# Where the tiles of a two-layer encoder trunk begin in SBUF: five pads changed

## The chip, the core and the metric

The kernel runs on one core of one Trainium2 chip, in one launch. The metric is the device time of that launch in microseconds (us); lower is better. The time before is 1945.97 us, the median of three runs that lie between 1945.92 and 1946.1 us.

The engines are called by the names of the profile: PE is TensorE (the matrix unit), PEld the load of its stationary operand, DVE is VectorE, ACT is ScalarE, POOL is GpSimd, SP is SyncE, which issues the loads of the weights. A matrix product has two operands in SBUF: the *stationary* one, 128 columns that are loaded into the array beforehand, and the *moving* one, whose columns (256, 288 or 512 here) stream past it. While one product streams, the stationary operand of the next is loaded.

## The reference

Two layers over 256 tokens of width 2048, all float32. Layer 0 mixes tokens by a convolution module, layer 1 by multi-head latent attention; each is followed by a squared-ReLU MLP of width 8192.

```python
def conv_module(h, w_pw1, b_pw1, w_dw, b_dw, ln_g, ln_b, w_pw2, b_pw2):
    u = h @ w_pw1 + b_pw1
    a, gate = jnp.split(u, 2, axis=-1)
    u = a * jax.nn.sigmoid(gate)
    u = lax.conv_general_dilated(u, w_dw[:, None, :].astype(u.dtype),
        window_strides=(1,), padding=[(CONV_WIDTH - 1, 0)], feature_group_count=D_MODEL, ...) + b_dw
    u = jax.nn.silu(layer_norm(u, ln_g, ln_b))
    return u @ w_pw2 + b_pw2

def mla(h, cos, sin, w_in, q_norm_g, kv_norm_g, w_q_up, w_kv_up, w_o):
    c_q, c_kv, k_pe = jnp.split(h @ w_in, [512, 1024], axis=-1)
    q = rms_norm(c_q, q_norm_g) @ w_q_up
    kv = rms_norm(c_kv, kv_norm_g) @ w_kv_up
    ...
    return o @ w_o

def sq_relu_mlp(h, w1, w2):
    return jnp.square(jax.nn.relu(h @ w1)) @ w2

def reference(x, positions, ...):
    for layer in range(2):
        h = rms_norm(x, norm_mixer_g[layer])
        x = x + (conv_module(h, ...) if layer == 0 else mla(h, ...))
        h = rms_norm(x, norm_mlp_g[layer])
        x = x + sq_relu_mlp(h, mlp_w1[layer], mlp_w2[layer])
    return rms_norm(x, final_norm_g)
```

The depthwise convolution is 31 taps wide and looks back only. The attention has 16 heads with 128 + 64 query and key dimensions, of which the 64 are rotated by position, and 128 value dimensions; a token sees the tokens up to the end of its own chunk of 64.

## The kernel before, in words

**Three products for one.** To keep float32 accuracy each operand is split into a high part (rounded to the format `F32R`) and a low part (the rest), and each product is made as high·high + low·high + high·low. `mm3` (L192) issues the three where the activations are stationary and the weights move (L194 high activations with high weights, L195 low activations with high weights, L196 high activations with low weights). Where the weights are stationary and the activations move, the three stand in the loops of the stage itself.

**Weights.** SP loads each block of weights into a tile `raw` (three buffers); ACT writes its high part into a tile `hi`, DVE (in the convolution mostly POOL) the low part into a tile `lo`, six buffers of each (`WB`), so the splitting runs ahead of PE by up to six tiles.

**Activations.** `xt` holds the turned (transposed) and normalised tokens, four tiles `xt_1` to `xt_4` in a pool on the right end of SBUF; for each block k of 128 features the high part of 256 tokens lies beside the low part of the same tokens. `sh` and `sl_` hold the gated, convolved and turned rows in the convolution module; the tiles `sh`/`sl` and `gh`/`gl` of an MLP hold its squared hidden values. In the attention, `kvh`/`kvl` and `qh`/`ql` hold the compressed keys and queries, `kTh`/`kTl`, `qTh`/`qTl`, `qpA`, `qpB`, `kpA`, `kpB` the keys and queries of a group of four heads, `vv` and `pT` values and softmax weights, `oh`/`ol` the heads' outputs.

**Stages, in order of time.**

1. The first convolution product (`conv_mm`, L841; L847 to L849): weights stationary, 256 columns of `xt` moving, 1536 products, in 16 rounds of 96. Around it, by a hand-written order, DVE makes the 31 taps of the depthwise convolution (L949), POOL splits weights (L169). Then LayerNorm.
2. The second convolution product (L1169, then `product_A`): `sh`/`sl_` stationary, 512 columns of weights moving, 384 products.
3. The MLP of layer 0. Up: weights stationary, L509 moves `xhl(k)`, the 512 columns of both parts of `xt`, past the high weights, L507 moves the 256 columns of the high part past the low weights; 16 of each for 128 hidden features. Down: `sh`, `sl`, `gh`, `gl` stationary, 512 columns of weights moving (L194 to L196), partly in a form with seven block products in place of eight. The hidden width is cut into four quarters; the first quarter's up products run alone, then down products of one quarter alternate with up products of the next (`ORDERS`), and the last quarter's down products run alone.
4. The attention. Its first product makes `ckv` in two blocks of 288 columns (`NKV`, L1590) and then `cq` in one of 512 (L1604), with `xt` stationary. The products with `kvh`, `kvl`, `qh`, `ql` follow (256 columns; stationary or moving), the scores (L1515 to L1517), the values, and the output product with `oh`/`ol` stationary (512 columns).
5. The MLP of layer 1, and the last normalisation.

**Addresses.** Each pool lays its tiles one behind the other, so a pad, a tile that nothing reads, moves what is behind it. All `hi` and `lo` tiles begin at 64 modulo 256 bytes, and so do the slices of 128 or 512 columns that the products take from them. The right pools (`xt`, and in the attention `gp` with the keys, queries and values of the heads) end below `pad_right`, so its size sets where they begin. The numbers of the pads are counts of float32, 4 bytes each.

Of the kernel before, what the change touches and what calls it, by code (L numbers as in the profile page):

```python
# [10 lines left out]
F32 = mybir.dt.float32  # L11
# [7 lines left out]
P = 128  # L19
# [16 lines left out]
PARTS = 4  # L36
PAD_CONST = 24
PAD_SMALL = 32
PAD_RIGHT = 48
PAD_KV = 8  # L40
PAD_O = 56
WB = 6
LOOK = WB // 2 - 1
LAST_PE = 22
# [37 lines left out]
def trunk_kernel(  # L82
# [26 lines left out]
    nc = tc.nc  # L109
# [22 lines left out]
    edge = ctx.enter_context(tc.tile_pool(name="edge", bufs=1, side="right"))  # L132
    pad_right = edge.tile([P, PAD_RIGHT], F32, name="pad_right")
    nc.gpsimd.memset(pad_right, 0.0)
# [658 lines left out]
    with ExitStack() as cx:  # L793
        cv = cx.enter_context(tc.tile_pool(name="cv", bufs=1, reuse_waits="tile"))
# [12 lines left out]
        b2 = cv.tile([P, D], F32, name="b2")  # L807

        cn = cv.tile([P, T, D], F32, tag="tok", name="cn")
        sh = cv.tile([P, KC, S], F32R, name="sh")  # L810
        sl_ = cv.tile([P, KC, S], F32R, name="sl_")
        stats = cv.tile([P, T, KC // 2, 6], F32, name="stats")

        UC = 2
# [429 lines left out]
    with ExitStack() as cx:  # L1244
        at = cx.enter_context(tc.tile_pool(name="at", bufs=1, reuse_waits="tile"))
# [92 lines left out]
                if h == 1:  # L1338
                    u_load(u + 3)

        pad_kv = at.tile([P, PAD_KV], F32, name="pad_kv")
        nc.gpsimd.memset(pad_kv, 0.0)
        kvh = at.tile([P, KR // P, S], F32R, name="kvh")
        kvl = at.tile([P, KR // P, S], F32R, name="kvl")
        qh = at.tile([P, QR // P, S], F32R, name="qh")
# [15 lines left out]
        for i in range(2):  # L1361
            for j in range(HG):
                nc.scalar.activation(qpB[i][DR:, j, :], mq[DR:, :], AF.Copy)
        pad_o = at.tile([P, PAD_O], F32, name="pad_o")
        nc.gpsimd.memset(pad_o, 0.0)
# [413 lines left out]
```

## Time and profile before

| | |
|---|---|
| median of 3 runs | 1945.97 us |
| the profiled execution's own time | 1946.03 us |
| its span, first to last instruction | 1944.2 us |
| PE busy | 1919.3 us, 99% of the span, 10778 products |
| DVE busy | 1652.7 us, 85% |
| ACT busy | 1206.4 us, 62% |
| POOL busy | 223.9 us, 12% |
| granted clock of PE | 0.999 |
| loaded from HBM | 363.68 MB, 188 GB/s over the span |

The profile is one execution. A row of the groups of instructions gives how many there are, their busy time, and the mean length of one in nanoseconds. Products overlap in the array: a product of 512 columns is shown as some 390 ns long, though the next one starts after some 230 ns. So two numbers are of use: the distance from one start to the next in the timeline, and the difference between the shown lengths of two groups. Around the span the execution has 1.8 us.

### The profile page before, as it was taken

How to read it: one execution, taken by the hardware profiler on the slowest of the kernel's cores; microseconds unless marked ns; L12 is line 12 of the kernel's file. 1: busy time of each engine (PE TensorE's matmuls, PEld its weight loads, DVE VectorE, ACT ScalarE, POOL GpSimd, SP SyncE). 2: the span in 40 equal slices, each digit the busy share in tenths (PEclk: the TensorE clock that was granted, in tenths of full speed). 3: DMA queues.
4: the chain of work that ended last, by engine and by line, in shares of the span. 5: the costliest groups of instructions: out<-in, count | busy, mean ns of one | idle time of the engine just before them, and what ended most of it. 6: DMA issues, size and time to landing. Idle time of an engine off the chain costs nothing.

```text
span 1944.2 us, 28476 instructions
## 1 busy us (share of the span) xinstructions
PE 1919.3 (99%) x10778; PEld 1675.2 (86%) x10778; DVE 1652.7 (85%) x2372; ACT 1206.4 (62%) x1709; POOL 223.9 (12%) x184
## 2 busy tenths in 40 slices
PE   7999999999999999999999999999999999999998
PEld 7999888888888888888899998888888888888886
DVE  5999865789999999999976665657999999999887
ACT  5556654766666666666566665566666666666654
POOL 5999400000000000000001410000000000000000
PEclk9999999999999999999999999999999999999999
DMA  8666355856666667666645445765667666666663
GB/s 237 182 179 191 130 195 154 231 168 206 204 195 206 196 201 210 197 199 211 200 145 180 119 149 174 208 181 172 196 195 209 203 195 196 213 199 194 209 223 108
DMA packets 407113, 367.62 MB, mean 189 GB/s; under 512 B 15416, under 2 KB 351936, under 8 KB 406720
## 3 DMA queue, kind: packets, MB, share of 16 engines
q1 hardware_dynamic: 405952, 363.63, 62.4%
q10 hardware_dynamic: 1024, 2.17, 0.3%
q8 instruction: 84, 1.38, 0.3%
q14 instruction: 53, 0.43, 0.1%
HBM read 363.68 MB, written 2.10 MB: 188 GB/s over the span
## 4 chain that ended last, share of the span: by engine, by line
PE 96%; DVE 1%; ACT 1%; POOL 1%; DMA 1%; issue 0%; DVEq 0%; ACTq 0%; POOLq 0%
PE acc L509 25%; PE acc L194 15%; PE acc L195 15%; PE acc L196 15%; PE acc L507 12%; PE acc L849 3%; PE acc L848 3%; PE acc L847 3%; PE acc L250 1%; PE sum L897 1%; PE acc L1547 0%; POOL lo L169 0%; DMA xs<-in_x 0%; ACT hi L168 0%; PE acc L1411 0%
## 5 line engine op out<-in xcount | busy, mean ns | idle before, releaser
L420 DVE TENSOR_TENSOR lo<-raw,hi 128x1024 fp32r<-128x1024 f32 (+1 forms) x512 | 571.2, 1122 | 91.4 <-ACT hi L419 90.8
L419 ACT ACTIVATE hi<-raw 128x1024 fp32r<-128x1024 f32 (+1 forms) x512 | 479.7, 970 | 67.8 <-PE acc L195 67.3
L509 PE MATMUL acc<-xt,hi 128*128 128x512 f32 x2048 | 512.8, 396 | 0.0
L509 PEld LDWEIGHTS acc<-xt,hi 128*128 128x128 f32 x2048 | 375.6, 188 | 79.3
L194 PE MATMUL acc<-hi,sh 128*128 128x512 f32 x930 | 363.4, 391 | 0.0
L196 PE MATMUL acc<-lo,sh 128*128 128x512 f32 x930 | 362.2, 390 | 0.0
L195 PE MATMUL acc<-hi,sl 128*128 128x512 f32 x802 | 312.0, 389 | 0.0
L507 PEld LDWEIGHTS acc<-xt,lo 128*128 128x128 f32 x2048 | 260.2, 188 | 11.7
L507 PE MATMUL acc<-xt,lo 128*128 128x256 f32 x2048 | 262.5, 281 | 0.0
L168 ACT ACTIVATE hi<-raw 128x1024 fp32r<-128x1024 f32 (+2 forms) x184 | 180.0, 1005 | 46.9 <-PE acc L195 41.7
L196 PEld LDWEIGHTS acc<-lo,sh 128*128 128x128 f32 x930 | 174.6, 188 | 37.0
L194 PEld LDWEIGHTS acc<-hi,sh 128*128 128x128 f32 x930 | 174.6, 188 | 36.7
L169 DVE TENSOR_TENSOR lo<-raw,hi 128x1024 fp32r<-128x1024 f32 (+2 forms) x118 | 133.2, 1148 | 68.7 <-ACT hi L168 62.9
L419 ACT ACTIVATE hi<-V 128x1024 fp32r<-128x1024 f32 x94 | 99.6, 1059 | 127.3 <-DVE V L715 124.0
L195 PEld LDWEIGHTS acc<-hi,sl 128*128 128x128 f32 x802 | 150.6, 188 | 31.4
L949 DVE SCALAR_TENSOR_TENSOR sum<-ub,w_dw,sum 128x256 f32<-128x256 f32 x400 | 162.8, 480 | 7.6 <-ACT sum L905 6.5
L169 POOL TENSOR_TENSOR lo<-raw,hi 128x1024 fp32r<-128x1024 f32 x66 | 157.7, 2414 | 23.9 <-ACT hi L168 23.9
L514 ACT ACTIVATE U<-acc 128x512 f32<-128x512 f32 x128 | 76.2, 595 | 131.2 <-PE acc L509 130.9
L419 ACT ACTIVATE hi<-T 128x1024 fp32r<-128x1024 f32 x94 | 99.3, 1056 | 85.7 <-DVE T L703 79.9
L847 PE MATMUL acc<-xt,hi 128*128 128x256 f32 x512 | 145.3, 284 | 0.0
L848 PE MATMUL acc<-xt,hi 128*128 128x256 f32 x512 | 143.9, 281 | 1.0 <-DVE xt L207 1.0
L849 PE MATMUL acc<-xt,lo 128*128 128x256 f32 x512 | 144.0, 281 | 0.0
(270 smaller groups left out, 2797.4 us busy)
## 6 DMA issues: line engine op xcount, KB each, us to landing
raw<-in_mlp_w SPq DMA_DIRECT2D x256, 1024.0 KB, 6.1
raw<-in_conv_w_pw SPq DMA_DIRECT2D x64, 512.0 KB, 5.5
raw<-in_conv_w_pw SPq DMA_DIRECT2D x16, 1024.0 KB, 5.0
raw<-in_mla_w_o SPq DMA_DIRECT2D x16, 1024.0 KB, 5.3
raw<-in_mla_w_kv_up SPq DMA_DIRECT2D x8, 1024.0 KB, 5.4
raw<-in_mla_w_in SPq DMA_DIRECT2D x8, 576.0 KB, 3.8
raw<-in_mla_w_in SPq DMA_DIRECT2D x4, 1024.0 KB, 6.5
raw<-in_mla_w_q_up SPq DMA_DIRECT2D x16, 256.0 KB, 4.7
```

The costliest lines, as they stand in the source:

```text
L168: nc.scalar.activation(hi, raw[:, js, :], AF.Copy)
L169: eng.tensor_tensor(lo, raw[:, js, :], hi.bitcast(F32), op=ALU.subtract)
L194: nc.tensor.matmul(ps, sh, mh, start=start, stop=False)
L195: nc.tensor.matmul(ps, sl, mh, start=False, stop=False)
L196: nc.tensor.matmul(ps, sh, ml, start=False, stop=stop)
L419: nc.scalar.activation(parts[0], src, AF.Copy)
L420: nc.vector.tensor_tensor(parts[1], src, parts[0].bitcast(F32), op=ALU.subtract)
L507: nc.tensor.matmul(ps[0][:, :S], wl[:, j, :], xh(k), start=False, stop=False)
L509: nc.tensor.matmul(ps[0], wh[:, j, :], xhl(k), start=k == 0, stop=k == KC - 1)
L847: nc.tensor.matmul(o, wh[:, bs], xh(k), start=k == 0, stop=False)
L848: nc.tensor.matmul(o, wh[:, bs], xl(k), start=False, stop=False)
L849: nc.tensor.matmul(o, wl[:, bs], xh(k), start=False, stop=k == KC - 1)
```

## The change

Five pads change; no line that computes anything does.

```diff
-PAD_RIGHT = 48
-PAD_KV = 8
-PAD_O = 56
+PAD_RIGHT = 40
+PAD_SH = 16
+PAD_STATS = 48
+PAD_O = 64
...
         cn = cv.tile([P, T, D], F32, tag="tok", name="cn")
+        cv.tile([P, PAD_SH], F32, name="pad_sh")
         sh = cv.tile([P, KC, S], F32R, name="sh")
         sl_ = cv.tile([P, KC, S], F32R, name="sl_")
+        cv.tile([P, PAD_STATS], F32, name="pad_stats")
         stats = cv.tile([P, T, KC // 2, 6], F32, name="stats")
...
-        pad_kv = at.tile([P, PAD_KV], F32, name="pad_kv")
-        nc.gpsimd.memset(pad_kv, 0.0)
         kvh = at.tile([P, KR // P, S], F32R, name="kvh")
         kvl = at.tile([P, KR // P, S], F32R, name="kvl")
         qh = at.tile([P, QR // P, S], F32R, name="qh")
```

The first attention product's blocks of one width, 288 and 288, stand in the kernel before as they do in the changed one. What each tile's address is in the two built programs, modulo 256 bytes:

| tiles | begin before | begin after |
|---|---|---|
| `hi`, `lo` (weights), `sh`/`sl`/`gh`/`gl` of the MLPs, `oh`, `ol` | 64 | 64 |
| `xt` (all four) | 32 | 64 |
| `sh`, `sl_` of the convolution | 0 | 64 |
| `kvh`, `kvl`, `qh`, `ql`, `kpA`, `kpB`, `qpB0`, `qpB1` | 96 | 64 |
| `kTh`, `kTl`, `qTh`, `qTl`, `qpA`, `vv`, `pT` | 32 | 64 |
| everything behind `stats` in the convolution | as it was (moved by 256 bytes) | as it was |

In the `ckv` product the second block of 288 columns of weights begins 1152 bytes behind the first, at 192 modulo 256, in both kernels.

Engine by engine the instructions stand in the same order with the same waits in the two programs. POOL alone differs: it clears a pad of 40 columns for one of 48 at the start, and one pad of 64 columns in the attention in place of two of 8 and 56.

## The prediction

> **What bounds the kernel.** I read the page's busy times and chain first, then the timeline of PE at one place of each stage, then the groups of products by shape. In the last instruction's chain PE is nearly everything:
>
> ```profile
> PE 1919.3 (99%) x10778; PEld 1675.2 (86%) x10778; DVE 1652.7 (85%) x2372; ACT 1206.4 (62%) x1709; POOL 223.9 (12%) x184
> PE 96%; DVE 1%; ACT 1%; POOL 1%; DMA 1%; issue 0%; DVEq 0%; ACTq 0%; POOLq 0%
> PE tr L290 <- DMA stage<-in_conv_b_dw: 12.0, 1, 12.0
> PE acc L1538 <- DVE pr L1532: 1.1, 2, 1.0
> ```
>
> Of PE's waits (who waited for whom, us, times, longest) the first is at the start, and none of the others comes to more than 1.1 us. So what counts is the distance at which products follow each other, and the timeline shows that equal products do not follow at equal distance. In the MLP of layer 0, down products are followed by up products:
>
> ```profile
> 704.74 0.39 PE L194 MATMUL acc<-hi,sh 128*128 128x512 f32 x1
> ...
> 707.23 0.39 PE L196 MATMUL acc<-lo,sh 128*128 128x512 f32 x1
> 707.46 2.03 PE L509 MATMUL acc<-xt,hi 128*128 128x512 f32 x8
> 709.33 2.05 PE L507 MATMUL acc<-xt,lo 128*128 128x256 f32 x16
> 711.21 1.09 PE L509 MATMUL acc<-xt,hi 128*128 128x512 f32 x4
> ```
>
> Twelve down products of 512 columns take 707.46 - 704.74 = 2.72 us, 226.7 ns each; eight up products of 512 columns take 1.87 us, 234 ns; sixteen of 256 columns take 1.88 us, 117.5 ns. In the chain in order of time sixteen of L509 make pieces of 3.73 us, 233.1 ns each, which I use:
>
> ```profile
> 323.20 3.73 PE acc L509 x16
> ```
>
> The groups by shape, over the whole run (lines, names, shapes, count, busy us, mean ns), say with what the distance goes:
>
> ```profile
> L509 PE MATMUL acc<-xt,hi 128*128 128x512 f32 x2048 | 512.8, 396 | 0.0
> L507 PE MATMUL acc<-xt,lo 128*128 128x256 f32 x2048 | 262.5, 281 | 0.0
> L195 PE MATMUL acc<-hi,gl 128*128 128x512 f32 x128 | 49.8, 389 | 0.0
> L195 PE MATMUL acc<-hi,ol 128*128 128x512 f32 x128 | 49.8, 389 | 0.0
> L195 PE MATMUL acc<-hi,xt 128*128 128x512 f32 x32 | 12.6, 395 | 0.0
> L195 PE MATMUL acc<-kTh,qTl 128*128 128x256 f32 x16 | 4.5, 278 | 0.0
> L1516 PE MATMUL acc<-kpA,qpA 128*128 128x256 f32 x16 | 4.5, 280 | 0.0
> L196 PE MATMUL acc<-kTl,qTh 128*128 128x256 f32 x16 | 4.5, 280 | 0.0
> L194 PE MATMUL acc<-kTh,qTh 128*128 128x256 f32 x16 | 5.3, 334 | 0.0
> L194 PE MATMUL acc<-hi,kvh 128*128 128x256 f32 x64 | 18.3, 286 | 0.0
> ```
>
> The three rows of L195 with 512 columns are the same instruction at the same line with the same moving tile `hi`; only the stationary tile differs. `gl` and `ol` begin at 64 modulo 256 bytes like the weights and stand at 389 ns, `xt` begins at 32 and stands at 395. L509 has the roles exchanged, `xt` moving past `hi`, and stands at 396. So what goes with the longer distance is neither the role nor the line but the start of one operand against that of the other: 6 ns on a product of 512 columns, in the shown length and in the distance alike. That is what the change alters.
>
> **The change part by part.** Nothing is added to the path: the instructions and their order stay, POOL clears one pad less, in a stage where it works 37.92 of 112 us (row below). I sum against the profiled execution's 1946.03 us, which is 0.06 us above the median.
>
> *The up products L509*: from 233.1 to 226.7 ns, the distance of the down products whose operands begin alike. 2048 of them by 6.4 ns are **13.1 us**. This is the firm term, since 512 columns with equal starts are seen in three tiles.
>
> *The up products L507*, 256 columns: 117.5 ns now, shown length 281 ns. No steady stretch of before has 256 columns with equal starts. Bounds: half of the distance of 512, 113.3 ns, would save 4.2 ns; on the other side the row of `hi` moving past `kvh` stands at 286 ns, 5 ns worse. The nearest rows are those of the scores: there `kTh` and `kTl` (at 32) move while `qTh` and `qpA` (at 32) are loaded, and `kpA` while `qpB` is (both at 96), equal starts at 278, 280 and 280 ns (the 334 ns of `kTh` past `qTh` are those of the first product behind a chain of 128 columns, of which each load is longer than the product; I leave it out). I take some 279.5 ns as the value: 1.5 ns, 2048 times, **3.1 us** (ends: 8.6 us saved, 10.2 us lost).
>
> *The second convolution product*, `sh` and `sl_` from 0 to 64, and *the query product* with `xt` stationary:
>
> ```profile
> 307.79 0.39 PE L194 MATMUL acc<-hi,sh 128*128 128x512 f32 x1
> ...
> 311.22 0.39 PE L194 MATMUL acc<-hi,sh 128*128 128x512 f32 x1
> ```
> ```profile
> 1035.81 0.39 PE L194 MATMUL acc<-hi,xt 128*128 128x512 f32 x1
> ...
> 1037.91 0.60 PE L250 MATMUL acc<-ident,ckv 128*128 128x128 f32 x4
> ```
>
> Fifteen products in 3.43 us are 228.7 ns, nine in 2.10 us are 233.3 ns. Brought to 226.7: 2.0 ns by 384 and 6.6 ns by 96, **0.8 and 0.6 us**.
>
> *The `ckv` product*, 288 columns, 192 of them:
>
> ```profile
> 1011.82 0.29 PE L194 MATMUL acc<-hi,xt 128*128 128x288 f32 x1
> ...
> 1014.90 0.30 PE L196 MATMUL acc<-lo,xt 128*128 128x288 f32 x1
> ```
>
> Twenty-three in 3.08 us, 133.9 ns; 288/512 of 226.7 would be 127.5. Only the first block's weights come to begin where `xt` does, the second's stay 128 bytes off. I take half, **0.6 us** (0 to 1.2).
>
> *The other attention products* of 256 columns, 752 by the groups' counts: their rows stand at 278 to 286 ns, those with equal starts at 278 to 280, so I take **nothing** (3.2 us saved at 113.3 ns, 3.8 us lost at 5 ns each).
>
> *The first convolution product*, 1536 of 256 columns, would save 2.3 us by the 1.5 ns above. But there PE is not alone:
>
> ```profile
> 20.00:206.00 186.00, 185.95 (x1572) 185.56 (x1571) 174.02 (x441) 106.96 (x180) 173.80 (x112) 1.00 0.66 185
> 100.00:150.00 50.00, 50.00 (x426) 50.00 (x425) 50.00 (x130) 26.51 (x42) 47.26 (x32) 1.00 0.67 182
> DVE sum L949 <- ACT sum L905: 6.5, 3, 4.5
> PE sum L897 <- DVE ub L872: 1.1, 1, 1.1
> ```
>
> The first two rows give, for a stretch, its length and the busy time of PE, PEld, DVE, ACT and POOL; the others who waited for whom, in us. From 100 to 150 us DVE is busy all the time with taps, POOL 47.26 of 50 us with splits. The stage ends when both PE and DVE have ended, and PE then already waits for DVE. A faster PE would only wait there more; what it can give is the time that DVE waited early in the stage, 6.5 us at the most. I take **0.5 us** (0 to 3.5: half of that wait, since part of it is the very first round).
>
> Could DVE take the gain of the MLPs too? It splits the weights there:
>
> ```profile
> 320.00:995.00 675.00, 675.00 (x3448) 574.62 (x3447) 613.94 (x739) 434.81 (x543) 0.25 (x2) 1.00 0.65 195
> 650.00:700.00 50.00, 50.00 (x266) 42.87 (x265) 49.73 (x61) 31.71 (x39) 0.00 (x0) 1.00 0.67 200
> 1048.00:1160.00 112.00, 110.88 (x924) 109.34 (x923) 76.62 (x173) 71.90 (x177) 37.92 (x56) 1.00 0.45 137
> ```
>
> It is busy 613.94 of 675 us. An MLP would get shorter by (13.1 + 3.1) / 2 = 8.1 us, so DVE would be at 613.94 / 667, 92%. One stretch of 50 us is at 49.73 already, but the six tiles of lead carry a few us of it. The loads of weights are at 0.65 of the engines' time, 195 GB/s, and need 1.2% more. I take no loss, and keep this as a rival.
>
> The sum: 13.1 + 3.1 + 0.8 + 0.6 + 0.6 + 0.5 = 18.7 us, 1946.03 - 18.7 = **1927 us**.
>
> [...]
>
> **The rivals.**
>
> *All products gain in proportion* (256 columns go to 113.3 ns). For it: 117.5 is half of 234, so off starts cost per column; then equal starts should too. Against it: the score rows at 278 to 280 ns, though these are short chains between products of 128 columns. 13.1 + 8.6 + 0.8 + 0.6 + 1.2 + 3.2 + 3.5 = 31 us: 1915 us.
>
> *DVE takes back what the mixed quarters gain.* Three of four quarters of up products alternate with down products, where DVE is at up to 49.73 of 50 us. If nothing is gained there, 1536 times 6.4 and 1.5 ns, 12.1 us, fall away: 6.6 us are left, 1939 us. Against it: PE shows no wait for DVE in either MLP, and 61 us of 675 are idle on DVE.
>
> *The starts do not matter* and 395 against 389 comes with the tile for another reason (its place far away in SBUF, what ACT and DVE do meanwhile): 1946 us. Against it: `sh` of the convolution at 0 lies between the two, at 228.7 ns, in a quiet stage.
>
> *Slower: equal starts hurt the products of 256 columns.* The stationary operand of the next product is loaded while one streams; with 256 columns the load fills nearly the whole stream (PEld is 185.56 of 186 us in the first convolution product, 574.62 of 675 in the MLP), so the two reads run side by side all the time, and equal starts might meet where the shift of 32 bytes kept them apart. The price is that of the row at 286 ns: 5 ns for 2048 + 752 + 1536 products (PE would bound the convolution again) is 21.7 us, against 14.5 saved at 512 columns: 1953 us. It decides from 14.5 / 4336 = 3.3 ns. [...] Against it: with equal starts no row of 256 columns is above 280, but for the first of a chain.
>
> **How the numbers follow.** Forecast 50%, in proportion 22%, DVE takes back 10%, no effect 6%, slower 12%. A difference of 0.2%, 3.9 us, is about what a measurement here can tell from none; the first three are faster by more, so faster 0.82, within 0.06, slower 0.12. The range leaves out no effect and slower, 18%: from 1911 (the proportional case, with the convolution giving back its whole 6.5 us) to 1942 (DVE takes back, and `ckv`, the convolution and L507 in the first quarters, 0.6 + 0.5 + 0.8 us, give nothing).
>
> **What would show it.** Right: L509 at 389 to 390 ns and sixteen of it in 3.63 us; L195 with `xt` at 389; L194 to L196 of the second convolution product at 389; L507 at 279 to 280. The proportional case shows 276 or 277 there; the slower one 284 or more. DVE's taking back would show as waits of PE at L507, L509 or L194 for DVE `lo`. The first convolution product should end at 205 to 206 us whatever its products do, with PE waiting for POOL or DVE before. Wrong altogether if L509 stays at 395.

## The result, and the profile after

The changed kernel takes 1940.74 us (median of 9 runs, 1940.63 to 1940.81), the kernel before 1945.95 us in the runs beside them: 0.9973 of the time, interval 0.9963 to 0.9983. So 5.2 us are gained where 18.7 were forecast. The direction was right, the range (1911 to 1942) held the time, the predicted 1927 us did not come.

The changed kernel's text has one line more ahead of `mm3` and three more ahead of the convolution product, so L194, L195, L196, L507, L509, L847 and L872 of before are L195, L196, L197, L508, L510, L850 and L875 now. Behind the convolution and ahead of the attention's products two lines fell away, so L1436 in the rows below is L1435 of before, where it stood at 279 ns. In the text I use before's numbers unless a row is quoted.

The page of the profile after, first PE's row of the busy times, then the shares of the chain that ended last; behind them PE's longest waits (who waited for whom, us, times, longest):

```profile
PE 1915.4 (99%) x10778; PEld 1682.5 (87%) x10778; DVE 1651.8 (85%) x2372; ACT 1204.8 (62%) x1709; POOL 223.7 (12%) x183
PE 98%; DVE 1%; DMA 1%; ACT 0%; issue 0%; DVEq 0%; ACTq 0%
PE tr L291 <- DMA stage<-in_conv_b_dw: 12.0, 1, 12.0
PE sum L900 <- DVE ub L875: 1.1, 1, 1.1
```

PE is still the bound, and no wait has taken the place of anything. What counts is again the distance from product to product. The groups by shape (line, names, shapes, count, busy us, mean ns):

```profile
L510 PE MATMUL acc<-xt,hi 128*128 128x512 f32 x2048 | 503.2, 391 | 0.0
L196 PE MATMUL acc<-hi,gl 128*128 128x512 f32 x128 | 49.8, 389 | 0.0
L196 PE MATMUL acc<-hi,xt 128*128 128x512 f32 x32 | 12.5, 391 | 0.0
L508 PE MATMUL acc<-xt,lo 128*128 128x256 f32 x2048 | 265.7, 283 | 0.0
L1436 PE MATMUL acc<-ql,hi 128*128 128x256 f32 x64 | 18.1, 283 | 0.0
```

The rows with 512 columns that stood at 395 or 396 ns came down, though to 391, not to the 389 of `gl`. The row of 256 columns went *up*, from 281 to 283. The timeline of PE says why (start us, us, line, count). First a place where up products follow down products:

```profile
706.25 0.39 PE L197 MATMUL acc<-lo,sh 128*128 128x512 f32 x1
706.48 1.98 PE L510 MATMUL acc<-xt,hi 128*128 128x512 f32 x8
708.29 2.08 PE L508 MATMUL acc<-xt,lo 128*128 128x256 f32 x16
710.20 2.00 PE L510 MATMUL acc<-xt,hi 128*128 128x512 f32 x8
```

Eight of 512 columns take 708.29 - 706.48 = 1.81 us, by the single starts 226.7 ns each, exactly the down products' distance. Then a place where up products of 512 columns follow up products of 256, once whole and once with the window begun later, so that the rows split:

```profile
324.51 3.82 PE L510 MATMUL acc<-xt,hi 128*128 128x512 f32 x16
328.17 2.08 PE L508 MATMUL acc<-xt,lo 128*128 128x256 f32 x16
...
325.67 2.66 PE L510 MATMUL acc<-xt,hi 128*128 128x512 f32 x11
328.17 0.28 PE L508 MATMUL acc<-xt,lo 128*128 128x256 f32 x1
...
328.52 1.72 PE L508 MATMUL acc<-xt,lo 128*128 128x256 f32 x13
330.08 0.40 PE L510 MATMUL acc<-xt,hi 128*128 128x512 f32 x1
```

The first five of 512 columns take 325.67 - 324.51 = 1.16 us, 232 ns each, the other eleven 2.50 us, 227 ns. By the starts of single products the five stand at 233.3, 235.8, 228.3, 232.5 and 230.8 ns, and from then on every one at 226.7: five products cost 27 ns together when the width changes from 256 to 512. Of the products of 256 columns, the last thirteen take 330.08 - 328.52 = 1.56 us, 120.0 ns each; the first behind the change stands at 113.3, the second at 119.2.

The `ckv` product, 288 columns:

```profile
1012.87 0.30 PE L195 MATMUL acc<-hi,xt 128*128 128x288 f32 x1
...
1014.47 0.30 PE L195 MATMUL acc<-hi,xt 128*128 128x288 f32 x1
```

Twelve in 1.60 us are 133.3 ns. Half of them take the second block of weights, which begins 128 bytes off `xt`, and stand at the same distance as the others. So with equal starts there is a rhythm that products fall into and keep. I call it **in step**: 226.7 ns for 512 columns, 120.0 for 256, 133.3 for 288 (there with only every second group of three at equal starts). The three lie on one line: 106.7 ns for each 256 columns and 13.3 ns for each product, the same at these three widths. Before, off step, 256 columns stood at 118.0, which is less.

The first convolution product is in step too. The last seventeen distances, and the stretch of the stage (length, then busy time of PE, PEld, DVE, ACT, POOL):

```profile
206.18 0.28 PE L850 MATMUL acc<-xt,hi 128*128 128x256 f32 x1
...
208.22 0.28 PE L852 MATMUL acc<-xt,lo 128*128 128x256 f32 x1
20.00:208.00 188.00, 188.00 (x1571) 187.82 (x1570) 174.99 (x441) 107.35 (x181) 174.19 (x112) 1.00 0.66 183
```

2.04 us for 17 is 120.0 ns; before, the stage's products stood at 118.4 on average. PE has no idle time left in the stage, and its last product starts at 208.2 us where it started at 206.1.

From the starts of the stages' first and last products in the two traces:

| stage, us | before | after | difference | forecast |
|---|---|---|---|---|
| first convolution product, to its end | 206.1 | 208.2 | +2.1 | -0.5 |
| second convolution product, LayerNorm | 112.4 | 111.8 | -0.6 | -0.8 |
| MLP of layer 0 | 677.9 | 674.3 | -3.6 | -8.1 |
| `ckv` and `cq` | 51.0 | 50.4 | -0.6 | -1.2 |
| rest of the attention | 110.5 | 111.4 | +0.9 | 0 |
| output product | 99.7 | 99.7 | 0 | 0 |
| MLP of layer 1 | 677.2 | 673.7 | -3.5 | -8.1 |
| sum | | | -5.3 | -18.7 |

In the MLPs L509 went from 233.3 to 228.6 ns on average (2048 times 4.7, -9.6 us) and L507 from 118.0 to 119.5 (+3.1 us); of the remaining 0.6 us, 0.5 are the down products'. Before, the first of them behind L509 stood at 232.9 ns by its start, some 6 ns above 226.7, at 86 such changes in the run; after, it stands at 226.7.

### The profile page after: what moved, and what is told of

Same layout as the page of the kernel before. It is cut to its first block, busy times and chain, and to the rows that moved or that the text cites. A ratio compares the mean times of both kernels' runs of the same rounds, so it can differ in the third digit from the quotient of the medians.

```text
span 1938.9 us, 28476 instructions
## 1 busy us (share of the span) xinstructions
PE 1915.4 (99%) x10778; PEld 1682.5 (87%) x10778; DVE 1651.8 (85%) x2372; ACT 1204.8 (62%) x1709; POOL 223.7 (12%) x183
## 4 chain that ended last, share of the span: by engine, by line
PE 98%; DVE 1%; DMA 1%; ACT 0%; issue 0%; DVEq 0%; ACTq 0%
PE acc L510 24%; PE acc L196 15%; PE acc L195 15%; PE acc L197 15%; PE acc L508 13%; PE acc L851 3%; PE acc L850 3%; PE acc L852 3%; PE acc L251 1%; PE sum L900 1%; PE acc L1435 0%; PE acc L1437 0%; PE acc L1436 0%; PE acc L1412 0%; PE acc L1414 0%; PE acc L1413 0%
## 5 line engine op out<-in xcount | busy, mean ns | idle before, releaser
L510 PE MATMUL acc<-xt,hi 128*128 128x512 f32 x2048 | 503.2, 391 | 0.0
L510 PEld LDWEIGHTS acc<-xt,hi 128*128 128x128 f32 x2048 | 376.1, 188 | 72.5
L195 PE MATMUL acc<-hi,sh 128*128 128x512 f32 x930 | 362.7, 390 | 0.0
L197 PE MATMUL acc<-lo,sh 128*128 128x512 f32 x930 | 362.0, 389 | 0.0
L196 PE MATMUL acc<-hi,sl 128*128 128x512 f32 x802 | 312.0, 389 | 0.0
L508 PEld LDWEIGHTS acc<-xt,lo 128*128 128x128 f32 x2048 | 262.6, 191 | 10.0
L508 PE MATMUL acc<-xt,lo 128*128 128x256 f32 x2048 | 265.7, 283 | 0.0
L197 PEld LDWEIGHTS acc<-lo,sh 128*128 128x128 f32 x930 | 174.6, 188 | 36.2
L195 PEld LDWEIGHTS acc<-hi,sh 128*128 128x128 f32 x930 | 174.6, 188 | 36.0
L196 PEld LDWEIGHTS acc<-hi,sl 128*128 128x128 f32 x802 | 150.5, 188 | 31.2
L850 PE MATMUL acc<-xt,hi 128*128 128x256 f32 x512 | 146.3, 286 | 0.0
```

The lines of the kernel that those rows point to most:

```text
L195: nc.tensor.matmul(ps, sh, mh, start=start, stop=False)
L196: nc.tensor.matmul(ps, sl, mh, start=False, stop=False)
L197: nc.tensor.matmul(ps, sh, ml, start=False, stop=stop)
L508: nc.tensor.matmul(ps[0][:, :S], wl[:, j, :], xh(k), start=False, stop=False)
L510: nc.tensor.matmul(ps[0], wh[:, j, :], xhl(k), start=k == 0, stop=k == KC - 1)
L850: nc.tensor.matmul(o, wh[:, bs], xh(k), start=k == 0, stop=False)
```

## The experiments

All kernels compute the whole result. Each was timed against the kernel before; behind a time stands its ratio to that kernel's, with the 95% interval in brackets. The times, with the mean distances of L507 and L509 and the start of the last convolution product, are gathered at the end of this section.

**One pad alone, four values.** Where the right pools begin, that is `xt` and in the attention the heads' keys, queries and values:

```diff
-PAD_RIGHT = 48
+PAD_RIGHT = 40
```

(e1: `xt` at 64; e2: 56, at 0; e3: 32, at 96; e4: 8, at 192.)

> Only PAD_RIGHT goes from 48 to 40, so xt and the attention's right pool begin at 64 like the weights; sh stays at 0, kvh at 96. Theory A (equal starts put every product into one step, 226.7 ns at 512 columns and 120.0 at 256, that is 106.7 ns for 256 columns and a fixed 13.3 ns for each product): L507 at 119.5 ns and L509 at 228.6 from start to start as in the changed kernel, first convolution product 2 us later than before, 1941.3 us (1940.3 to 1942.3). Theory B (most of the expected gain went in the other parts, sh and kvh, and xt alone gives what was forecast): 1931 us or less.

1940.54 us, 0.9972 [0.9959, 0.9984]: all of the change's gain comes from `xt`, and so do the 119.5 ns of L507 and the 228.6 ns of L509. (The heads' tiles moved as well, but the rest of the attention takes 110.6 us for 110.5.) That the other pads took the missing 13 us back falls.

> Only PAD_RIGHT goes from 48 to 56: xt at 0 modulo 256, 64 bytes off the weights. Theory A (the difference of the starts decides): not in step; L509 near the 228.7 ns that the second convolution product has with sh at 0, L507 near 117 ns, 1936 us (1932 to 1942), so L507 is below 119 ns. Theory C (what counts is a start at a multiple of 64 bytes, not the weights'): the same as with xt at 64, L507 at 119.5 ns, L509 at 228.6, 1941 us.

1938.12 us, 0.9958 [0.9939, 0.9978]. With `xt` 64 bytes ahead of the weights L507 goes to 114.0 ns, as the theory of the difference of the starts wants; that multiples of 64 bytes are all alike falls. But L509 stayed at 233.2 ns, which I had not expected. In the chain in order of time (start, us, what):

```profile
324.08 3.74 PE acc L509 x16
327.82 1.82 PE acc L507 x16
```

L507's gain of 4 ns is 8.2 us, and the two MLPs got shorter by 3.6 and 3.7 us. What is missing went at the changes from L509 to down products: the first three of these take 20 ns more than in step, 86 times, 1.7 us, against 0.5 us before. The convolution product ended 5.2 us earlier, at 200.9 us, and yet the MLP began at 319.4, 0.9 us *later* than before. PE stood waiting for a tap's product of DVE:

```profile
PE sum L897 <- DVE ub L872: 4.3, 1, 4.3
205.46 8.00 PE L897 MATMUL sum<-ub,dg 128*128 128x256 f32 x22 [4.25 <-DVE ub L872]
201.00:206.00 5.00, 0.75 (x3) 0.52 (x3) 5.00 (x15) 1.98 (x4) 3.23 (x3) 0.87 0.33 134
206.00:211.00 5.00, 5.00 (x13) 3.90 (x12) 5.00 (x14) 3.04 (x5) 4.43 (x4) 0.50 0.01 3
```

In the kernel before, the same 22 products, and the same stretch:

```profile
207.53 5.02 PE L897 MATMUL sum<-ub,dg 128*128 128x256 f32 x22 [1.15 <-DVE ub L872]
206.00:211.00 5.00, 3.85 (x20) 3.24 (x19) 4.47 (x13) 4.52 (x8) 3.98 (x5) 1.00 0.37 148
```

The seventh number of a stretch, behind POOL's, is the granted clock: 0.50 from 206 to 211 us in e2, 1.00 before. DVE is busy all 5.00 us of both stretches of e2, so a faster PE only reached DVE's end earlier and idled 4.3 us. Behind that wait, at a clock of 0.50 and from 211 to 216 us of 0.95, it needed 8.00 us for the 22 products that took 5.02 before, where PE had waited 1.15 us ahead of them. These are two waits with a clock beside each; that the wait lowered the clock they do not show by themselves.

> Only PAD_RIGHT goes from 48 to 32: xt at 96, 32 bytes off the weights on the other side than before. Theory A: L509 near 233 ns as with the query product's stationary xt 32 bytes off, L507 near 117 ns as L1436 with qh at 96: 1944 us (1941 to 1947). Theory C: as before, 1946 us, L509 at 233.3 and L507 at 118.0 ns.

1946.57 us, 1.0001 [0.9990, 1.0012]: no gain, L509 at 233.3 ns. For it 32 bytes behind the weights are as bad as 32 ahead. The eight runs spread more than any other kernel's, from 1944.78 to 1946.93 us, and the trace is of the lowest; why they do is not known. In the trace the convolution product ends at 203.8 us, 2.3 us earlier than before, PE then waits 2.1 us for DVE's tap at a granted clock of 1.00, and the MLP begins 1.4 us earlier.

> Only PAD_RIGHT goes from 48 to 8: xt at 192, 128 bytes off the weights. In the changed kernel the second block of 288 columns of the ckv product, 128 bytes off its stationary xt, is as slow as the first (133 ns). Theory A with a period of 256 bytes: not in step, L507 below 119 ns, L509 between 228 and 234, 1934 to 1944 us. Theory A with a period of 128 bytes: in step as with xt at 64, L507 at 119.5, L509 at 228.6 ns, 1941.3 us.

1950.04 us, 1.0021 [1.0010, 1.0032]: slower than before. That starts count modulo 128 falls for 256 and 512 columns (L507 at 118.8, L509 at 232.8 ns, neither in step); my own theory's 1934 to 1944 was a miss as well. The down products, whose operands did not move, lost the most: by their starts the first nine behind L509 take 47 ns more than in step, 86 times, 4.0 us, against 0.5 us before. L507 lost 1.5 us and L509 gained 1.0, together about the 4.1 us by which the MLPs got longer.

**The change without `xt`.** The changed kernel with `PAD_RIGHT` back at 48.

> All of the change but PAD_RIGHT: sh and sl_ at 64, kvh and its neighbours at 64, xt and the right pool left at 32. Theory A: the second convolution product gains 0.6 to 0.8 us, the products of 256 columns with kvh and qh go from 117 to 120 ns and lose 1 us: 1946 us (1945.3 to 1946.9). Theory B (these parts bring, the shift of xt takes away): below 1944.

1946.49 us, 1.0002 [0.9991, 1.0014], as expected: the second convolution product gives its 0.6 us (111.8), the attention's products of 256 columns take 1.0 back (111.5 against 110.5).

**Each stage with what suits it.** If 256 columns do better off step and 512 in step, `xt` should lie at 32 while the convolution product runs and at 64 from the MLP on, and the attention's `kvh` to `ql` at 96 as before.

```diff
-PAD_O = 64
+PAD_KV = 8
+PAD_O = 56
...
-    open_xt("xt0")
+    open_xt("xt0", 8)
...
+        open_xt("xt0b")
...
+        pad_kv = at.tile([P, PAD_KV], F32, name="pad_kv")
+        nc.gpsimd.memset(pad_kv, 0.0)
```

(The argument of `open_xt` is a pad behind the four tiles in a pool that ends at a fixed place, so the tiles begin 32 bytes earlier; the second call opens the pool again behind the convolution.)

> The changed kernel, but xt at 32 during the first convolution product and at 64 from the first MLP on (the pool is opened once more in between, with a pad of 8 behind it the first time), and kvh and its neighbours back at 96. Theory A: that stage ends 2 us sooner, the attention is 0.9 us shorter, MLPs as changed: 1938 us (1937 to 1939.5). Rival (the first convolution stage is DVE's: what PE gains there is waited away): 1939.8 us.

1937.87 us, 0.9958 [0.9939, 0.9978], as expected. The convolution product ends at 206.2 again, the attention takes 110.6 again: those two losses of the change are the 120.0 ns of 256 columns in step.

**The low weights elsewhere.** All `lo` tiles at 128, the rest at 64, so that L507's products would find their own difference of -64: the moving tile begins 64 bytes ahead of the stationary one that is loaded meanwhile.

```diff
-PAD_SMALL = 32
+PAD_LO = 16
+PAD_SMALL = 16
...
+        if not lo_pads:
+            lo_pads.append(wpool.tile([P, PAD_LO], F32, tag="pad_lo", name="pad_lo", bufs=1))
```

> The changed kernel with all lo tiles 64 bytes further, at 128 (a pad of 16 before them, PAD_SMALL 16 for 32), so what is loaded next decides apart: hi equal to xt, lo 64 bytes behind it. Theory A (the moving operand's start minus that of the operand loaded meanwhile decides; e2 had -64 for L507): L507 at 114.1 to 115 ns while L509 stays near 228 ns; down products whose weights are lo (L197) at 229; 1940.7 - 11 + 2.4 = 1932 us (1928 to 1937). Theory D (the place of xt in SBUF by itself made e2's L507 quick): L507 stays at 119.5 ns, 1941 to 1943 us.

1952.58 us, 1.0033 [1.0017, 1.0049]: slower, neither theory's time. L507 stood at 117.9 ns, not 113.4, and the down products lost what they had (L200 and L201 are L194 and L195 there):

```profile
L200 PE MATMUL acc<-hi,sh 128*128 128x512 f32 x930 | 367.6, 395 | 0.0
L201 PE MATMUL acc<-hi,sl 128*128 128x512 f32 x802 | 315.1, 393 | 0.0
```

L200 moves `hi` while a stationary tile at the same start is loaded, and yet it rose from 390 to 395 ns (by the starts in the MLPs, from 226.7 in the changed kernel to 232.7); of the three products one, `lo`, has unequal starts. So in e7 a product's distance was not a matter of its own two operands alone; the sequence as a whole had fallen out of step.

**Twice as many changes of width.** Up products as 8 high, 8 low, 8 high, 8 low in place of 16 and 16 (the mark of the last product of a sum moves with the order, not shown):

```diff
-                        for low in (h, 1 - h):
+                        for low in (0, 1):
```

> The changed kernel with the up products of the second half in the order of the first, L509 before L507, so that 256 columns are followed by 512 twice in a unit of 128 hidden features in place of once (the second time the next unit's or the down products follow). In the changed kernel the first five products of 512 columns behind one of 256 cost 27 ns more than in step, and the first of 256 behind 512 costs 6.7 ns less. Theory E (coming back into step costs that much at each change of width): 128 times 20.7 ns more, 1943.4 us (1942.5 to 1944.5), L509's mean 228 to 229 ns, and L195 to L197 behind L508 above 227. Rival F (it goes with the second half's tiles, not with the change of width): 1940.7 us.

1943.41 us, 0.9986 [0.9975, 0.9997], the 1943.4 that the cost of the change of width gives. In the chain:

```profile
323.79 1.84 PE acc L510 x8
325.63 0.95 PE acc L508 x8
326.58 1.84 PE acc L510 x8
```

Eight behind 256 columns take 1.84 us, eight behind down products took 1.81 in the profile after: 27 ns for each of 128 changes more, less the 7.5 ns by which the first two products of each run of 256 columns stay below 120.0, is 2.5 us; measured are 2.7.

**512 in step and 256 at -64.** The up products' low weights alone at 64 bytes behind all else, by a place of their own in the `lo` tiles; everything else at 0 (e9) or at 64 (e10).

```diff
+UP_AT = 16
...
-                        parts[h] = [a.rearrange("p a (j n) -> p (a j) n", n=P) for a in hi_lo(2)]
+                        parts[h] = [a.rearrange("p a (j n) -> p (a j) n", n=P) for a in hi_lo(2, UP_AT)]
```

> All tiles of the changed kernel 64 bytes earlier (PAD_CONST 8 for 24, PAD_RIGHT 56 for 40), so xt, hi, lo, sh, gh, oh and kvh begin at 0 modulo 256; lo tiles get 256 bytes of room (taken from a scratch region that nothing uses), and the up products alone put their low weights 64 bytes into the tile, at 64. So L507's pair is that of e2 (xt at 0, lo at 64) and all others begin alike. Theory G (a difference of -64 bytes is quick when xt begins at 0, not when it begins at 64): L507 113.4 to 114 ns, L509 and the down products near 227 to 229 as changed, 1940.7 - 12 = 1928.5 us (1926 to 1932). Theory I (the quick state of e2 needs L509 off as well, since the two alternate): L507 at 117 to 119 ns, 1936 to 1940 us.

1936.76 us, 0.9952 [0.9933, 0.9972].

> The same without the shift of everything: xt, hi, lo, sh, gh, oh at 64 as in the changed kernel, the up products' low weights at 128. The difference for L507 is -64 bytes as in e2 and e9. Theory G: L507 at 117.7 ns as in e7 where xt and lo stood so, down products back at 227 to 229 ns, 1940.7 - 3.7 = 1937 us (1935.5 to 1939). Theory H (the difference alone decides, and e7's 117.7 came from its disturbed down products): L507 at 113.4 to 114 ns, 1928.5 us.

1937.39 us, 0.9957 [0.9937, 0.9976]. The two differ by 0.6 us, so where everything lies together hardly matters. But L507 came to 117.9 ns, not to e2's 113.4, at the same difference of starts. The groups from 330 to 980 us, e9 first (L516 is L507, L518 is L509), then e2:

```profile
L516 PE MATMUL acc<-xt,lo 128*128 128x256 f32 x992 | 127.1, 281 | 0.0
L518 PE MATMUL acc<-xt,hi 128*128 128x512 f32 x999 | 245.2, 391 | 0.0
```
```profile
L507 PE MATMUL acc<-xt,lo 128*128 128x256 f32 x992 | 123.2, 277 | 0.0
L509 PE MATMUL acc<-xt,hi 128*128 128x512 f32 x999 | 249.8, 395 | 0.0
```

In the MLPs, then, 256 columns settled at some 118 ns behind products in step in e9 and e10 and at 113.4 behind products off step in e2, and no kernel here has 391 and 277 together. But products of 512 columns are not needed for the two distances. In e2's first convolution product, all of 256 columns with every `hi` and `lo` at 64 and `xt` at 0, both stand in one stage. Two of its rounds (start, us, what), thirty products from the first row of a pair to the second:

```profile
64.10 0.28 PE L847 MATMUL acc<-xt,hi 128*128 128x256 f32 x1
...
67.50 0.28 PE L847 MATMUL acc<-xt,hi 128*128 128x256 f32 x1
```
```profile
75.98 0.28 PE L847 MATMUL acc<-xt,hi 128*128 128x256 f32 x1
...
79.51 0.28 PE L847 MATMUL acc<-xt,hi 128*128 128x256 f32 x1
```

These are 3.40 us, 113.3 ns each, and 3.53 us, 117.7 ns each. Of the twelve rounds from 62 to 197 us every third, four in all, stands at 117.7 ns and the other eight at 113.3. So one sequence with one set of starts modulo 256 keeps one of two distances through a whole round. A round takes four of the six buffers of `hi` and of `lo`, so every third one begins with the same buffers; whether that chooses the distance, or what PE did before, is not shown.

**Joined.** e9 with e6's places for the convolution and the attention; then the same with the up products' low weights at 192 in place of 64 (`UP_AT = 48`).

> e9 and e6 joined: all equal starts at 0, the up products' low weights 64 bytes into their tile, xt 32 bytes before its weights (at 224) during the first convolution product alone, kvh and its neighbours at 32. If the parts add up, as theory A has it for e6 and the trace of e9 for L507: 1936.8 - 2.9 = 1933.9 us (1933 to 1935), the fastest so far. If the convolution's gain is taken back by DVE here: 1935.8 us.

1933.82 us, 0.9937 [0.9922, 0.9952], as expected: the fastest of all, 6.9 us below the changed kernel and 12.3 below the one before. Its chain in order of time (L521 is L509, L519 is L507):

```profile
322.06 3.65 PE acc L521 x16
325.71 1.89 PE acc L519 x16
327.60 3.65 PE acc L521 x16
```

> As the joined kernel, but the up products' low weights 192 bytes into their tile, so that xt begins 64 bytes behind them in place of 64 before (modulo 256). Theory A with a sign (the stationary tile 64 bytes before the moving one is not the same as behind: 228.7 against 233 ns at 512 columns): L507 at another distance than 117.7 ns, between 114 and 120, 1926 to 1939 us. Theory I (entered from products in step, L507 falls into the same state for any difference but 0): 117.5 to 118 ns, 1933.9 us.

1938.19 us, 0.9959 [0.9945, 0.9974], not the time of e11: L507 stood at 117.8 ns, as said, but the change of width became dearer. The same view:

```profile
325.80 1.89 PE acc L519 x16
327.69 3.69 PE acc L521 x16
```

Here ten products, not five, pass behind the 256 columns before 226.7 ns is reached (240.7, 237.4, 233.4, 235.6, 224.3, 230.9, 235.7, 228.4, 232.5, 230.6, by their starts): 62 ns together in place of 27, 4.5 us over 128 changes. On average over the kernel L509 is at 230.3.

| kernel | us | L507, ns | L509, ns | last convolution product, us |
|---|---|---|---|---|
| before (`xt` 32 ahead of the weights) | 1945.95 | 118.0 | 233.3 | 206.1 |
| after (equal) | 1940.74 | 119.5 | 228.6 | 208.2 |
| e1 (`xt` equal, other pads as before) | 1940.54 | 119.5 | 228.6 | 208.1 |
| e2 (`xt` 64 ahead) | 1938.12 | 114.0 | 233.2 | 200.9 |
| e3 (`xt` 32 behind) | 1946.57 | 117.5 | 233.3 | 203.8 |
| e4 (`xt` 128 off) | 1950.04 | 118.8 | 232.8 | 206.5 |
| e5 (the change without `xt`) | 1946.49 | 118.0 | 233.3 | 206.1 |
| e6 (a place for each stage) | 1937.87 | 119.5 | 228.6 | 206.2 |
| e7 (`lo` 64 behind) | 1952.58 | 117.9 | 229.2 | 205.5 |
| e8 (twice the changes of width) | 1943.41 | 119.1 | 229.2 | 208.3 |
| e9 (up products' `lo` 64 behind, rest at 0) | 1936.76 | 117.9 | 228.6 | 207.8 |
| e10 (the same, rest at 64) | 1937.39 | 117.9 | 228.5 | 208.2 |
| e11 (e9 and e6 joined) | 1933.82 | 117.9 | 228.5 | 205.6 |
| e12 (e11, up products' `lo` 192 behind) | 1938.19 | 117.8 | 230.3 | 205.7 |

The distances are means from each product's start to the next product's, over all 2048.

## Why the prediction was right and wrong

**The step that failed** is the value for L507: "I take some 279.5 ns as the value: 1.5 ns, 2048 times, 3.1 us". It came to 283 ns and a *loss* of 3.1 us, 6.2 us off, the largest single error. The value was read from the rows of the scores, the only ones of before with 256 columns and equal starts. But these are chains of few products between products of 128 columns, and the profile after shows that the first product behind another width stands at 113.3 ns and the later ones at 120.0: a short chain shows the start, not the steady distance. The same rows of the scores, at equal starts in both kernels, bear this out: by their starts the four behind the first of each chain stood at 115.6 to 117.8 ns on average before and stand at 117.3 to 118.6 after, none of the four at 120.0. (Of the products of 128 columns ahead of them four distances take 0.45 us in before, 1092.59 to 1093.04; they are shown as 274 to 276 ns long, their loads as 189 to 190. That the load is longer than the product there was an estimate of mine.) The prediction named these chains as short, in the rival, and took their number all the same. The result lies between the two bounds it gave (8.6 us saved, 10.2 lost); the choice between them was wrong.

**L509** was right in direction and off in size. Its 6.4 ns are there where it follows down products (226.7 ns from 706.48 to 708.29 us). Behind L507 five products come back into step only slowly, 27 ns each time, 128 times: 3.5 us of the 13.1. e8 doubled that cost and measured it. The step assumed that a product's distance depends on its own operands; in e7 down products with `hi` and `sh` at equal starts stood at 232.7 ns for 226.7, so there the sequence counted too.

**The first convolution product**: forecast 0.5 us saved, ended 2.1 us later. The size comes from the same wrong sign at 256 columns (120.0 for 118.4 ns, 1536 times, is 2.4 us). "It should end at 205 to 206 us whatever its products do" is wrong upwards, because a slower PE is the bound (188.00 of 188.00 us busy). Downwards the products do end sooner, and the stage passes little of it on, as the prediction had it: of e3's 2.3 us 1.4 arrived at the MLP, of e2's 5.2 us nothing.

**The attention products of 256 columns**, costed at nothing, lost 0.9 us, for the same reason; e5 and e6 show both directions. **The second convolution product** (0.6 for 0.8) and **`ckv` with `cq`** (0.6 for 1.2) came about as forecast; of `ckv`, 133.9 became 133.3 ns, in step, and not the 127.5 that I had set as its floor, since the 13.3 ns per product are the same at 256, 288 and 512 columns.

**The rivals.** In proportion: the 113.3 ns appeared, but as the first product of a run, and steadily only in e2, where the starts are *not* equal. DVE takes back: no wait of PE for `lo` in either MLP. It took back in the convolution alone, and only in e2 and e3. No effect falls: moving one pad by 32 bytes took 5.5 us off in e1. The slower rival had the sign at 256 columns right, with a price of 1.5 ns at L507 where 3.3 would have decided; that the two reads meet, its reason, is not shown. (By the prediction's own terms the ends of its range, 1911 and 1942, come to 1912 and 1941; nothing hangs on it.)

The gain that did not come is thus accounted for: 6.2 us at L507, 3.5 at L509, 2.6 in the convolution, 0.9 in the attention, 0.6 at `ckv` and `cq`, 0.2 in the second product; less the 0.6 us that the MLPs gained beside their up products, that is 13.4 us.

## What to carry to other kernels

A distance for a long run of products must be read from a long run of the same width: the first ones behind another width say something else (113.3 and 119.2 ns against 120.0 in the changed kernel), and their mean belongs to neither. Where addresses change the distance, find for each stage and width which start suits it (here equal starts for 512 columns, unequal for 256) and place each stage's operands by its own; one start for all gave 5.2 us, a start for each stage and one for the up products' low weights 12.3. And before a product is made faster in a stage where another engine ends last, look at PE's idle time and granted clock there (in e2 4.3 us of waiting, then a clock of 0.50 from 206 to 211 us).

## What was not expected of the hardware

- In step, a product cost 13.3 ns beyond 106.7 ns per 256 columns, at three widths (120.0, 133.3 and 226.7 ns in the changed kernel). At 256 columns being off step was cheaper (113.4 to 118.8 ns against 120.0), at 512 it was dearer (228.7 with `sh` at 0, some 233 with `xt` off, against 226.7). At 288 columns 128 bytes off made no difference (133.3).
- Coming into step at 512 columns took five products and 27 ns behind 256 columns with equal starts in the changed kernel, ten products and 62 ns in e12. Products whose own operands never moved paid it too: the down products behind L509 6 ns before, 20 in e2, 47 in e4.
- The same difference of starts has given two steady distances at 256 columns, 113.4 ns in e2's MLPs and 117.5 to 118.4 in e7, e9, e10 and e11; in e2's convolution product both stand side by side, 113.3 and 117.7. Why is open. Open is also what in the array or the memory makes the rhythm: that the load of the next stationary operand is what the moving one meets was argued from the addresses alone, and no run took the loads away.
- Behind 4.3 us of waiting the granted clock was 0.50 for a stretch of 5 us, and 22 products took 8.00 us, 3 us beside the wait (e2); behind 2.1 us it was 1.00 and they took 5.02 us (e3). Whether the wait decides the clock, no run shows.
